# One layer's expert stage: three blocks of row gathers ranked below a product, and 112 instead of 80 of its chunks listed ahead of the gates

## The chip, the cores and the metric

The kernel runs on one core of a Trainium2 chip. The metric is the device time of one execution in microseconds (us). A core has a matrix engine (TensorE, PE in the rows; PEld is its weight load), a vector engine (VectorE, DVE), a scalar engine (ScalarE, ACT), GpSimd (POOL) and a sync engine (SyncE, SP), each working through its own list of instructions in order, and 16 DMA engines that they share.

## The reference

Two layers work on 512 latent tokens and, in the first layer only, on 256 context tokens, of 1024 features. Each layer is a mixer (attention in layer 0, two recurrences in layer 1) and then a PEER expert layer with 16384 experts, of which each token takes 16 in each of 8 heads:

```python
def block(xb):                                  # 128 tokens
    q = (xb @ w_q).reshape(T, PEER_HEADS, 2, PEER_HALF)
    s = jnp.einsum("thpd,pkd->thpk", q, sub_keys)
    sv, si = lax.top_k(s, PEER_TOPK)
    ...
    top_s, pos = lax.top_k(cand_s, PEER_TOPK)   # 16 of the 16 x 16 sums
    idx = jnp.take_along_axis(cand_i, pos, axis=-1)
    gate = jax.nn.softmax(top_s, axis=-1)
    act = jax.nn.gelu(jnp.einsum("td,thkd->thk", xb, u[idx]), approximate=False)
    return jnp.einsum("thk,thkd->td", (gate * act), v[idx])
```

The context's last state starts the recurrences of layer 1.

## The kernel before

There are six blocks of 128 tokens in layer 0: two of context, four latent. The expert layer is computed in two ways. Three latent blocks (`DENSE`) take the **dense path**: for all 16384 experts, in 128 chunks of 128 experts, `hidden` makes u.x for the 384 tokens and a GELU (24 matmuls that write `ph`; per chunk one 512 KB load `u`, its split into two parts `uh` on ScalarE, L793, and `ul` on VectorE, L794), and `peer_values` multiplies by the gates and by v into six PSUM banks `acc` (18 matmuls, a 512 KB load `v` with its split `vh`, `vl`, and the split `wl` of the gated hidden). The gates of all experts are built by `gate_grid` out of the routing: per block 32 groups of four tokens, each with comparisons `oi` on VectorE, `oj` on VectorE and ScalarE by turns (ScalarE's in L772 and L775), four matmuls `pt`, an eviction `stage`, and a 1 MB store per 16 tokens.

The two context blocks and one latent block (`REST`) take the **gather path**, `gather_run`: 128 indirect loads of u rows (512 KB each, issued by GpSimd, L722), each followed by a dot product on VectorE (L724), and then 128 loads of v rows (L731), each followed by an accumulation on VectorE into `gacc` (L736). Row buffers `grow` are five in layer 0.

In `peer_lat` the first `128 - LATE[layer]` chunks of `hidden` are listed ahead of `gate_grid`. Their result goes to memory (`Hd`, 192 KB each) and is read back by `peer_values`. The remaining `LATE[layer]` chunks are made inside `peer_values`, which takes them first. When these are done, the memory of `hidden` is given back and `ctx_states` (the context's half of layer 1: norms, gates, features, then `delta_unit` and `delta_step`) is listed with a high rank, so that it runs beside the rest of `peer_values`. It needs both context blocks finished.

The order on each engine is made at build time by a scheduler that simulates a timeline: of what is ready it takes the one with the highest rank. `high_priority(offset=-BACK)` ranks all within it far below everything else; within one rank, what was written earlier goes first.

Of the kernel before, what the change touches and what calls it, by code (L numbers as in the profile page):

```python
# [11 lines left out]
F32R = mybir.dt.float32r  # L12
BF16 = mybir.dt.bfloat16
BACK = 1 << 20
LATE = [48, 0]
GH = 2
DENSE, REST = [1, 2, 3], [0]

# [32 lines left out]
class Kern:  # L51
# [823 lines left out]
    def peer_ctx(self, R):  # L875

        layer = 0
        with R("peer_c") as keep:
            xT = keep.tile([128, KD, CTX], F32, name="xT")
            with R("peer_n") as pn:  # L880
                self.norm_mod_T(pn, self.hc, xT, *self.acol[layer][1, 1], roles=("o", "a", "a"))
            with R("peer_r") as pool:
                kT = self.peer_keys(pool, layer)
                preps = [self.gather_prep(xT, b) for b in range(NC)]
                self.gather_select(pool, self.query(pool, layer, xT), kT, preps)
                for b in range(NC):
                    with self.tc.high_priority(offset=-BACK):
                        self.gather_run(layer, preps[b], self.hc[b], 1)

    def peer_open(self):  # L890
# [25 lines left out]
    def peer_lat(self, layer, meanwhile=None):  # L916

        nc, tc = self.nc, self.tc
        nd = len(DENSE)
        n = nd * 128  # L920
        Hd = tc.dram_tile([128, 128, n], F32, name=f"Hd{layer}")
        Gd = tc.dram_tile([16, 128, n // 16, 8, 16], F32, name=f"Gd{layer}")
        with ExitStack() as er:
            es = ExitStack()
            P = lambda nm, b=1, **k: es.enter_context(tc.tile_pool(name=nm, bufs=b, reuse_waits="tile", **k))
            R = lambda nm, b=1, **k: er.enter_context(tc.tile_pool(name=nm, bufs=b, side="right", reuse_waits="tile", **k))
            pu, ph = R("dn_u", 2), R("dn_h", 2, space=PSUM)
            self.pm = Banks(P("pp", 1, space=PSUM), {"a": ("pa", 2), "t": ("pt", 2), "o": ("po", 2)})
            (xh, xl), x0 = self.xs, self.x0
            pool, pq, pg = P("peer_r"), P("peer_q"), P("gg", 2)  # L930

            def project(hp):
                ps = self.pm("a")
                w = self.rows_x(pq, self.A["peer_w_q"][layer, hp], ps[:, :n], (xh, xl), (2, 1, 1))
                for k, b in enumerate(REST):
                    self.product(ps[:, n + k * 128:n + (k + 1) * 128], w, x0[b])
                return ps

            kT = self.peer_keys(pool, layer)
            preps = [self.gather_prep(x0[b], 0) for b in REST]  # L940
            sv = [pool.tile([128, 16, 16], F32, name=f"sv{b}") for b in range(NL)]
            si = [pool.tile([128, 16, 16], U32, name=f"si{b}") for b in range(NL)]

            def route(hp):
                g, r = divmod(hp, 2 * GH)
                if r == 2 * GH - 1:
                    self.gather_route(pool, sv[nd:], si[nd:], preps, g, g * GH)

            self.peer_scores(pool, project, kT, sv, si, route)
            with tc.high_priority(offset=-(1 + layer) * BACK):  # L950
                for b, prep in zip(REST, preps):
                    self.gather_run(layer, prep, self.h[b], 0)
            pw = R("dn_w", 2)
            ahead = 128 - LATE[layer]
            with tc.high_priority(offset=-BACK):
                for i in range(ahead):
                    w = pw.tile([128, n], F32, name="hw")
                    self.hidden(layer, i, w, pu, ph, (xh, xl))
                    nc.sync.dma_start(Hd[i], w)
            for k in range(nd):  # L960
                self.gate_grid(pg, Gd, k, *self.peer_route(pool, sv[k], si[k]))
            es.close()
            def hidden(i, w):
                if i < ahead:
                    nc.sync.dma_start(w, Hd[i])
                else:
                    self.hidden(layer, i, w, pu, ph, (xh, xl))

            y = self.peer_values(layer, Gd, Hd, [self.h[b] for b in DENSE], list(range(ahead, 128)) + list(range(ahead)),
                                 hidden)  # L970
            for i in range(128 - ahead):
                next(y)
        self.px.close()
        for _ in range(ahead):
            next(y)
        if meanwhile:
            next(y)
            with tc.high_priority(offset=3000):
                meanwhile()
            next(y, None)  # L980
        else:
            with tc.tile_pool(name="fin", bufs=NL, side="right", reuse_waits="tile") as pool:
                self.done = self.final_norm(pool)
                for b in REST:
                    self.done(self.h[b], b)
                next(y)
            next(y, None)
# [713 lines left out]
```

## Time and profile before

| | us |
|---|---|
| median of 3 runs | 4478.54 (4475.19 to 4487.54) |
| the profiled execution | 4486.37 |
| its span | 4484.6 |
| TensorE busy in it | 3977.4 (89%) |
| VectorE busy | 3428.2 (76%) |
| ScalarE busy | 1786.9 (40%) |
| GpSimd busy | 1546.6 (34%) |

The profile divides the span into 40 slices and names for each engine its busy share, the clock that was granted to TensorE, and how busy the DMA engines were. Times in the rows are counted from the start of the span. The stretches used below were cut at instructions: 1274 us is the first `oi` of layer 0's gates, 1442 the end of their first third, 1650 their end, 1677 the first `vl`, 1914, 2149 and 2331 each 32 chunks of `peer_values` on, 2495 the last `vl`.

### The profile page before, as it was taken

Reading aid. Unit: us, or ns where it says so; the run is one execution under the profiler, and the core shown is the slowest. Engines: PE = TensorE matmul, PEld = TensorE weight load, DVE = VectorE, ACT = ScalarE, POOL = GpSimd, SP = SyncE. Lnnn points to the kernel's source line nnn. Section 1 sums busy time; section 2 is a strip of 40 time slices with the busy share of each in tenths; the row PEclk is TensorE's granted clock in tenths of the full one; section 3 lists DMA queues with packets and bytes.
Section 4 is the critical chain, followed back from the end, with each engine's and each line's share of the span. In section 5 each row is a group of like instructions: output and inputs, shape, how many; then the busy total and the mean of one; then the engine's idle time right before and its main releaser. Section 6 shows DMA issues by size and latency. Waiting matters only on the chain. (4 is left out here: it accounts for less than half of the span.)

```text
span 4484.6 us, 63555 instructions
## 1 busy us (share of the span) xinstructions
PE 3977.4 (89%) x22484; PEld 3491.4 (78%) x22484; DVE 3428.2 (76%) x7022; ACT 1786.9 (40%) x3481; POOL 1546.6 (34%) x1252
## 2 busy tenths in 40 slices
PE   7995488798798559999999999998998899899998
PEld 5784265698798548997788768988987899888887
DVE  2349988899989988889975566674998888677555
ACT  3311144222346643334343433334333577433333
POOL 0026766655444554445530001221233334223000
PEclk9997598799999669999999999998999999999999
DMA  8748777988789999999985211122687899999765
GB/s 309 265 159 287 272 253 254 317 316 315 277 273 325 331 337 347 329 342 345 349 295 172 76 48 34 36 71 72 201 281 256 304 334 332 358 343 329 244 223 161
DMA packets 430455, 1140.21 MB, mean 254 GB/s; under 512 B 38148, under 2 KB 200324, under 8 KB 418872
## 3 DMA queue, kind: packets, MB, share of 16 engines
q1 hardware_dynamic: 280376, 574.04, 37.1%
q0 software_dynamic: 147456, 536.94, 34.4%
q10 hardware_dynamic: 2304, 25.17, 1.5%
q8 instruction: 177, 2.90, 0.3%
q14 instruction: 142, 1.16, 0.1%
HBM read 1039.01 MB, written 96.99 MB: 253 GB/s over the span
## 5 line engine op out<-in xcount | busy, mean ns | idle before, releaser
L731 POOL DMA_INDIRECT grow<-peer_v,gidx x512 | 722.6, 1411 | 833.1 <-DVE gacc L736 676.0
L722 POOL DMA_INDIRECT grow<-peer_u,gidx x512 | 663.6, 1296 | 697.4 <-DVE hid L724 433.4
L806 PE MATMUL ph<-xh,uh 128*128 128x384 f32 x2048 | 722.1, 353 | 106.6 <-ACT uh L793 84.4
L806 PE MATMUL ph<-xl,uh 128*128 128x384 f32 x2048 | 710.9, 347 | 0.6 <-DVE xl L124 0.6
L736 DVE SCALAR_TENSOR_TENSOR gacc<-grow,gw,gacc 128x1024 f32<-128x1024 f32 x508 | 658.2, 1296 | 42.3 <-DMA grow<-peer_v,gidx 38.6
L724 DVE CUSTOM_DVE_ANT_0 grow<-grow,gx 128x1024 f32<-128x1024 f32 x512 | 619.6, 1224 | 53.6 <-DMA grow<-peer_u,gidx 53.1
L793 ACT ACTIVATE uh<-u 128x1024 fp32r<-128x1024 f32 x340 | 357.8, 1056 | 509.2 <-DMA u<-peer_uT 185.4
L794 DVE TENSOR_TENSOR ul<-u,uh 128x1024 fp32r<-128x1024 f32 x340 | 415.6, 1224 | 118.3 <-ACT uh L793 95.7
L806 PEld LDWEIGHTS ph<-xh,uh 128*128 128x128 f32 x2048 | 402.4, 197 | 132.3 <-ACT uh L793 100.3
L841 PE MATMUL acc<-vl,wh 128*128 128x512 f32 x1536 | 481.9, 394 | 3.5 <-DVE vl L794 3.4
L841 PE MATMUL acc<-vh,wl 128*128 128x512 f32 x1536 | 474.9, 392 | 0.0
L841 PE MATMUL acc<-vh,wh 128*128 128x512 f32 x1536 | 422.2, 395 | 16.5 <-ACT vh L793 11.4
L808 PE MATMUL ph<-xh,ul 128*128 128x384 f32 x2048 | 409.3, 339 | 13.9 <-DVE ul L794 13.7
L806 PEld LDWEIGHTS ph<-xl,uh 128*128 128x128 f32 x2048 | 403.1, 197 | 4.4 <-DVE xl L124 1.0
L808 PEld LDWEIGHTS ph<-xh,ul 128*128 128x128 f32 x2048 | 360.0, 189 | 20.9 <-DVE ul L794 17.5
L794 DVE TENSOR_TENSOR vl<-v,vh 128x1024 fp32r<-128x1024 f32 x256 | 312.9, 1222 | 82.4 <-ACT vh L793 81.6
L793 ACT ACTIVATE wh<-w 128x384 fp32r<-128x384 f32 x256 | 134.3, 525 | 583.2 <-PE acc L841 418.2
L841 PEld LDWEIGHTS acc<-vh,wh 128*128 128x128 f32 x1536 | 287.7, 189 | 73.7 <-ACT vh L793 13.0
L780 PE MATMUL pt<-oi,oj 128*128 128x128 f32 x1536 | 243.5, 318 | 111.6 <-DVE oj L769 69.8
L841 PEld LDWEIGHTS acc<-vl,wh 128*128 128x128 f32 x1536 | 287.9, 189 | 65.5 <-DVE vl L794 6.3
L841 PEld LDWEIGHTS acc<-vh,wl 128*128 128x128 f32 x1536 | 288.8, 189 | 60.8
L793 ACT ACTIVATE vh<-v 128x1024 fp32r<-128x1024 f32 x256 | 270.8, 1059 | 141.8 <-PE acc L841 133.8
(549 smaller groups left out, 6601.0 us busy)
## 6 DMA issues: line engine op xcount, KB each, us to landing
u<-peer_uT SPq DMA_DIRECT2D x256, 512.0 KB
v<-peer_v SPq DMA_DIRECT2D x256, 512.0 KB
w<-mod_w SPq DMA_DIRECT2D x48, 1024.0 KB
Gd<-stage SPq DMA_DIRECT2D x48, 1024.0 KB
Hd<-hw SPq DMA_DIRECT2D x208, 192.0 KB
w<-Hd SPq DMA_DIRECT2D x208, 192.0 KB
u<-rec_w SPq DMA_DIRECT2D x52, 512.0 KB
g<-Gd SPq DMA_DIRECT2D x16, 1536.0 KB
```

The costliest lines, as they stand in the source:

```text
L722: nc.gpsimd.indirect_dma_start(out=u, out_offset=None, in_=A[f"peer_u{layer}"], in_offset=bass.IndirectOffsetOnAxis(ap=row(s), axis=0))
L724: nc.vector.tensor_tensor_reduce(u, u, x, 1.0, 0.0, OP.mult, OP.add, hid[:, s:s + 1])
L731: nc.gpsimd.indirect_dma_start(out=u, out_offset=None, in_=A[f"peer_v{layer}"], in_offset=bass.IndirectOffsetOnAxis(ap=row(s), axis=0))
L736: nc.vector.scalar_tensor_tensor(acc, u, w[:, s:s + 1], acc, op0=OP.mult, op1=OP.add)
L780: nc.tensor.matmul(ps[:, t * 128:(t + 1) * 128], oj[:, t], oi[:, t], start=True, stop=True)
L793: nc.scalar.activation(hi, x, AF.Copy)
L794: nc.vector.tensor_tensor(lo, x, hi.bitcast(F32), op=OP.subtract)
L806: self.nc.tensor.matmul(ps, wh[:, kd, :], b[:, kd, :], start=kd == 0 and b is xh, stop=False)
L808: self.nc.tensor.matmul(ps, wl[:, kd, :], xh[:, kd, :], start=False, stop=kd == KD - 1)
L841: nc.tensor.matmul(acc[b][f], a[:, b * 128:(b + 1) * 128], c[:, f * 512:(f + 1) * 512], start=k + t == 0, stop=k == len(chunks) - 1 and t ...
```

## The change

`LATE[0]` goes from 48 to 16, so 112 instead of 80 chunks of layer 0's `hidden` are listed ahead of the gates and pass through `Hd`. The gathers of the two context blocks and of layer 0's latent block get the rank `-2 * BACK`, below `hidden`; before, they had the rank of `hidden` and were written ahead of it. Layer 1 had that rank already and keeps it, and its `LATE` of 0.

```diff
-LATE = [48, 0]
+LATE = [16, 0]
 ...
                 for b in range(NC):
-                    with self.tc.high_priority(offset=-BACK):
+                    with self.tc.high_priority(offset=-2 * BACK):
                         self.gather_run(layer, preps[b], self.hc[b], 1)
 ...
             self.peer_scores(pool, project, kT, sv, si, route)
-            with tc.high_priority(offset=-(1 + layer) * BACK):
+            with tc.high_priority(offset=-2 * BACK):
                 for b, prep in zip(REST, preps):
                     self.gather_run(layer, prep, self.h[b], 0)
```

Counted in VectorE's list, layer 0:

| VectorE instructions | before | after |
|---|---|---|
| splits `ul` ahead of the first `oi` (16 of them of the queries) | 70 | 78 |
| from first to last `oi`: splits `ul` | 30 | 54 |
| from first to last `oi`: dot products and accumulations of gathers | 140 | 117 |
| gathers of the two context blocks ended at the last `oi` | all | all |
| dot products and accumulations of gathers after the first `vl` | 213 | 236 |
| chunks of `peer_values` begun when the last gather is accumulated | 96 | 128 |
| chunk of `peer_values` at which `ctx_states` begins | 49 | 17 |
| instructions of `ctx_states` on VectorE after the last `vl` | 83 | 22 |

VectorE in the third block of the gates, around the 72nd `oi` of 96 (`gacc` is the gathers' accumulation, `ul` the split of a chunk). Before:

```order
L769 TENSOR_TENSOR oj_13150<-oj_13150,tt_13070 128x512
L764 TENSOR_TENSOR oi_13170<-iota_112,tt_13070 128x512
L736 SCALAR_TENSOR_TENSOR gacc_3913<-grow_4265,gw_3910,gacc_3913 128x1024
L764 TENSOR_TENSOR oj_13178<-iota_112,tt_13070 128x512
L764 TENSOR_TENSOR oi_13181<-iota_112,tt_13070 128x512
L736 SCALAR_TENSOR_TENSOR gacc_3913<-grow_4268,gw_3910,gacc_3913 128x1024
```

After:

```order
L764 TENSOR_TENSOR oj_14266<-iota_112,tt_14158 128x512
L764 TENSOR_TENSOR oi_14269<-iota_112,tt_14158 128x512
L736 SCALAR_TENSOR_TENSOR gacc_3913<-grow_4241,gw_3910,gacc_3913 128x1024
L769 TENSOR_TENSOR oj_14266<-oj_14266,tt_14158 128x512
L794 TENSOR_TENSOR ul_12783<-u_12780,uh_12782 128x1024
L736 SCALAR_TENSOR_TENSOR gacc_3913<-grow_4244,gw_3910,gacc_3913 128x1024
L794 TENSOR_TENSOR ul_12817<-u_12814,uh_12816 128x1024
```

Splits of chunks stand between the comparisons, where only gathers stood.

VectorE around the 110th chunk of `peer_values` (`vl`, `wl` its splits, `w` the product with the gates, `tu` of `ctx_states`). Before:

```order
L794 TENSOR_TENSOR vl_18458<-v_18455,vh_18457 128x1024
L854 TENSOR_TENSOR w_18579<-w_18579,g8_18550 128x384
L1157 COPY_PREDICATED tu_20034<-tri_19072,pa_20170 128x32x4
L1179 COPY tu_20022<-pa_20174 128x256
L794 TENSOR_TENSOR wl_18494<-w_18484,wh_18493 128x384
L794 TENSOR_TENSOR vl_18489<-v_18486,vh_18488 128x1024
```

After:

```order
L794 TENSOR_TENSOR wl_18559<-w_18549,wh_18558 128x384
L736 SCALAR_TENSOR_TENSOR gacc_8679<-grow_8950,gw_8676,gacc_8679 128x1024
L794 TENSOR_TENSOR vl_18554<-v_18551,vh_18553 128x1024
L1179 COPY tu_20460<-pa_20682 128x256
L1179 COPY tu_20464<-pa_20689 128x256
L736 SCALAR_TENSOR_TENSOR gacc_8679<-grow_8953,gw_8676,gacc_8679 128x1024
L854 TENSOR_TENSOR w_18611<-w_18611,g8_18396 128x384
```

The last chunks had no gathers; now one or two accumulations stand in each.

VectorE at the end of `peer_values` (L870 adds it to `h`). Before:

```order
L870 TENSOR_TENSOR h2_102<-h2_102,v_19041 128x1024
L1219 TENSOR_TENSOR wd_20385<-pa_20380,gt1_19074 128x512
L869 TENSOR_TENSOR v_19057<-acc20_13552,v_19010 128x512
L869 TENSOR_TENSOR v_19057<-acc21_13553,v_19010 128x512
L1219 TENSOR_TENSOR wd_20392<-pa_20387,gt1_19074 128x512
L870 TENSOR_TENSOR h3_103<-h3_103,v_19057 128x1024
L1140 SCALAR_TENSOR_TENSOR nbt_20401<-pa_20394,gt6_19079,dec_20399 128x128 x2
```

After:

```order
L870 TENSOR_TENSOR h2_102<-h2_102,v_19137 128x1024
L869 TENSOR_TENSOR v_19153<-acc20_14640,v_19106 128x512
L869 TENSOR_TENSOR v_19153<-acc21_14641,v_19106 128x512
L736 SCALAR_TENSOR_TENSOR gacc_8679<-grow_9055,gw_8676,gacc_8679 128x1024
L870 TENSOR_TENSOR h3_103<-h3_103,v_19153 128x1024
L736 SCALAR_TENSOR_TENSOR gacc_8679<-grow_9058,gw_8676,gacc_8679 128x1024
L736 SCALAR_TENSOR_TENSOR gacc_8679<-grow_9061,gw_8676,gacc_8679 128x1024
```

The second half of `ctx_states` (`wd`, `nbt`) stood here; it is now ahead of this place, and the last accumulations of the latent block's gather have come here.

## Rows read from the trace of the kernel before

**Rows 1.** Windows: PE, PEld, DVE, ACT, POOL busy (count); granted clock, DMA share, GB/s.

```profile
953.00:1274.00 321.00, 270.29 (x1485) 260.39 (x1483) 308.75 (x1019) 101.41 (x137) 163.65 (x116) 0.95 0.84 298
1274.00:1442.00 168.00, 152.45 (x921) 148.79 (x920) 149.25 (x177) 100.31 (x211) 72.46 (x44) 0.96 0.90 304
1442.00:1650.00 208.00, 109.45 (x518) 100.76 (x518) 196.46 (x263) 126.24 (x325) 124.16 (x97) 0.66 0.98 330
1677.00:1914.00 237.00, 237.00 (x1189) 214.36 (x1188) 193.75 (x286) 87.14 (x117) 105.26 (x83) 1.00 0.94 342
1914.00:2149.00 235.00, 226.25 (x1135) 197.85 (x1134) 204.32 (x260) 97.34 (x158) 112.98 (x88) 0.97 0.94 346
2044.00:2149.00 105.00, 96.25 (x479) 79.85 (x478) 96.71 (x148) 51.45 (x97) 49.39 (x42) 0.93 0.97 365
2149.00:2331.00 182.00, 176.42 (x921) 147.40 (x920) 162.32 (x203) 73.13 (x118) 87.96 (x62) 1.00 0.93 338
2331.00:2495.00 164.00, 162.99 (x860) 138.36 (x859) 90.14 (x154) 63.92 (x108) 3.32 (x4) 1.00 0.49 155
2503.00:2601.00 98.00, 79.70 (x487) 69.89 (x485) 61.12 (x135) 44.43 (x121) 2.64 (x14) 0.91 0.19 60
3600.00:3800.00 200.00, 189.96 (x1228) 184.39 (x1226) 172.97 (x219) 152.42 (x353) 75.94 (x56) 1.00 1.00 340
```

**Rows 2.** Windows of tile `grow` (gathers): DVE busy (count), POOL busy (count), clock, DMA.

```profile
1442.00:1650.00 208.00, 121.62 (x97) 124.16 (x97) 0.66 0.98 330
1914.00:2149.00 235.00, 99.14 (x78) 110.79 (x79) 0.97 0.94 346
2149.00:2331.00 182.00, 68.98 (x54) 84.11 (x48) 1.00 0.93 338
3600.00:3800.00 200.00, 68.95 (x55) 75.94 (x56) 1.00 1.00 340
```

**Rows 3.** Windows of tile `ul` (splits): PE, PEld, DVE busy (count), clock, DMA.

```profile
1274.00:1442.00 168.00, 43.94 (x225) 38.96 (x224) 36.66 (x30) 0.96 0.90 304
1914.00:2149.00 235.00, 31.14 (x164) 27.45 (x164) 23.19 (x19) 0.97 0.94 346
2149.00:2331.00 182.00, 13.48 (x96) 12.38 (x96) 14.68 (x12) 1.00 0.93 338
3600.00:3800.00 200.00, 51.26 (x255) 43.30 (x253) 37.84 (x31) 1.00 1.00 340
```

**Rows 4.** Window of tile `ph` (hidden): PE, PEld, ACT busy (count), clock, DMA.

```profile
1677.00:1914.00 237.00, 118.24 (x648) 113.56 (x646) 13.17 (x27) 1.00 0.94 342
```

**Rows 5.** Window of tile `acc` (values): PE, PEld, DVE busy (count), clock, DMA.

```profile
1677.00:1914.00 237.00, 129.26 (x541) 101.24 (x542) 0.00 (x0) 1.00 0.94 342
```

**Rows 6.** Windows of tile `oi` (gates): PE, PEld, DVE busy (count), clock, DMA.

```profile
1442.00:1650.00 208.00, 108.17 (x512) 99.69 (x512) 44.09 (x65) 0.66 0.98 330
3600.00:3800.00 200.00, 62.90 (x471) 59.83 (x471) 38.99 (x57) 1.00 1.00 340
```

**Rows 7.** Waits in 1442:1650: who waited for whom, us in total, times, longest.

```profile
PEld pt L780 <- ACT oj L775: 67.8, 23, 4.3
```

**Rows 8.** Groups by line, PE, in 2503:2601: busy, mean ns | idle before.

```profile
L806 PE MATMUL pa<-aTl,uh 128*128 128x512 f32 x64 | 17.0, 416 | 0.0
...
L808 PE MATMUL pa<-aTl,ul 128*128 128x512 f32 x32 | 8.5, 396 | 0.0
...
L107 PE MATMUL pa<-cm,xn 128*128 128x128 f32 x16 | 3.8, 387 | 0.0
```

**Rows 9.** Timeline of PE behind the last chunk: start us, us, instruction, idle before.

```profile
2549.50 5.03 PE L806 MATMUL pa<-aTl,uh 128*128 128x512 f32 x16
...
2601.16 6.30 PE L806 MATMUL pa<-aTl,wgh 128*16 128x512 f32 x16 [4.71 <-ACT xp L1018]
```

**Rows 10.** The page, sixth part: DMA issues, with KB each.

```profile
u<-peer_uT SPq DMA_DIRECT2D x256, 512.0 KB
...
w<-Hd SPq DMA_DIRECT2D x208, 192.0 KB
```

## The prediction

> **What bounds the kernel now.** I read the windows first, stage by stage, because the busy shares of the whole span (TensorE 89%, VectorE 76%) average over stages with different limits. Layer 0's expert stage shows three of them [rows 1]. The scores (953 to 1274) are VectorE's: 308.75 us busy of 321, 96%. The gates fall into two parts. In their first third (1274 to 1442) 30 chunks of the dense path run beside them [rows 3] and TensorE is busy for 152.45 of 168 us at a clock of 0.96. [...] Then `peer_values` (1677 to 2495, 818 us) is TensorE's: 237, 226.25, 176.42 and 162.99 us, together 802.7 or 98%, while VectorE has 193.75 + 204.32 + 162.32 + 90.14 = 650.5 us and the DMA engines run at 0.93 to 0.94 of their time until the gathers end at about 2331, and at 0.49 behind that. The change takes TensorE's work from the stage that it bounds to one where it idles. Whether that pays is decided by VectorE and DMA, which are nearly full in both.
>
> **The change part by part.** *What a chunk costs TensorE.* In 1677 to 1914 it never idles, and holds 648 matmuls of `ph` [rows 4] and 541 of `acc` [rows 5]: 27 chunks of 24. Their busy times overlap (118.24 + 129.26 = 247.5 in 237 us), so I scale them: 237 x 118.24 / 247.5 = 113.2 us, 4.2 a chunk. 32 chunks are 134 us; the ends are 4.0 (all the overlap taken off `ph`) and 4.4.
>
> *The rank.* It does less than it says. In VectorE's order both context blocks' gathers still end at the last comparison. What moves are 23 dot products and accumulations of the latent block, from the gates (140 to 117) into `peer_values` (213 to 236), where they reach to the last chunk. Ahead of the scores nothing moves at all. One costs VectorE 68.98 / 54 = 1.28 us [rows 2] and moves 512 KB (0.524 MB).
>
> *Scores, +8.5 us.* 8 more splits at 36.66 / 30 = 1.22 us [rows 3], less one gather, on a VectorE that is full [rows 1]. If its waits took them in, 0.
>
> *Gates, +17 us.* The first third keeps 30 splits and loses one gather: 168 us as before. In the rest, 24 splits (29 us) replace 22 gathers (28 us): VectorE keeps its 196 us, and if it kept its pace the stretch would keep its 208. TensorE takes 24 x 4.2 = 101 us for 98.5 idle ones; but its 512 gate matmuls cost 108.17 us there and 471 of the same kind 62.90 where the clock was 1.00 [rows 6], so at full clock it needs 68 + 101 = 169 of 208. ScalarE gets 24 evictions and splits onto 126.24 us; in the stretch of layer 1 below it carried 152.42 of 200. DMA gets 24 loads and stores of 512 + 192 KB [rows 10], 17.3 MB, for 11.5 MB of gathers: 5.8 MB, 17 us at the 330 GB/s of this stretch, which is at 0.98. The nearest row with all of it together is layer 1's 3600 to 3800: in 200 us it does 57 of the comparisons [rows 6], 31 splits [rows 3] and 55 gathers [rows 2], with VectorE at 172.97, DMA at 1.00 and the clock at 1.00. This stretch has 64, 24 and about 75: 64 / 57 x 200 = 225 us, in which 11 splits too many and 13 gathers too few nearly cancel (13.4 against 16.6 us of VectorE). I take 225, +17, between 0 (VectorE's pace kept) and +34 (if a DMA that is full there cannot hide the 17 us of additional bytes either). Each chunk also puts two transfers into SyncE's queue between the gate stores, which wait for ScalarE; the loads behind them are buffered two deep, as in the first third, where TensorE still was 91% busy.
>
> *`peer_values`, -61 us.* Three floors for the whole of it. TensorE: 802.7 - 134 + 50 (the part of `ctx_states` that comes in, below) = 719. VectorE: 650.5 - 39 + 29 + 31 (about half of its 61.12 in 2503 to 2601) = 672. DMA: 237 x 342 + 235 x 346 + 182 x 338 + 164 x 155 = 249.3 MB [rows 1], less 32 loads of `u`, more 32 reads of `Hd` and 23 gathers, 250.9 MB: 734 us at 342 GB/s. That rate is not a ceiling, since 2044 to 2149 shows 365, and so I let TensorE's 719 be the low end. [...]
> Against floors I set the stretches that already look like the new ones. Chunks 1 to 32 now hold 15 chunks of hidden, 67 gathers and the start of `ctx_states`: as 1914 to 2149 did (19 splits, 78 gathers, 235 us), less four splits' products and 11 gathers: 220. Chunks 33 to 64 hold 12 splits and 55 gathers, as 2149 to 2331 (12 and 54, 182 us): 183. The last two lots of 32 look like 2331 to 2495 (164 us, TensorE full) with 54 gathers each: VectorE 90.14 + 69 = 159 us, which is 97% of 164, and 179 at the 89% that 2149 to 2331 reached; DMA 25.4 + 28.3 = 53.7 MB, 157 us. I take 177 each. Sum 757, -61; the bounds are -99 (719 us) and -13 (235 + 190 + 190 + 190).
>
> *Behind the last chunk, -22 us.* From 2503 to 2601 TensorE is busy 79.70 us; the products of layer 1 take 17.0 + 8.5 and the norms' transposes twice about 3.8 [rows 8], so about 46, with the overlaps up to 50, are the second half of `ctx_states`, which now runs ahead. What is left is a chain: norms until the first product at 2549.5, 25.5 us of products, and then the gates' product, which came at 2601.16 behind a wait of 4.71 [rows 9]. Without the rest: 46.5 + 25.5 + 4 = 76 of 98. The bounds are 0 (the norms set it alone) and -46. The latent block's last six accumulations come here now; three dense norms go ahead of that block's, which hides them. If they were late, they would cost 6 x 1.28 = 8 us.
>
> *Layer 1* keeps its code and, but for a few neighbours changed, its order: 0, within 10 us either way.
>
> **The sum.** 8.5 + 17 - 61 - 22 = -57.5 us on the profiled execution's 4486.4: 4428.9. That execution was 7.9 us above the median of the three runs, so from the median 4478.5 it is **4421**.
>
> **The rivals.** [...]
> *B, no difference: VectorE's order takes the bound.* Gathers now stand in every chunk, and each accumulation waits in line for its row. If VectorE got no further than the 82% of 1677 to 1914, `peer_values` would take 672 / 0.82 = 820 us: 8.5 + 17 + 2 - 22 = +5, 4484. Against it: in that stretch TensorE set the pace, and the next two show 87 and 89%. 11%.
> *C, more than forecast:* TensorE's floor is reached in `peer_values` (-99), the gates keep their 208 us, and the tail gives 35: 8.5 - 99 - 35 = -125, 4353. It needs VectorE at 94% for 719 us; 1442 to 1650 shows that share, but with TensorE half idle. 7%.
> *D, the tail stays:* `ctx_states` starts at chunk 17 by the list, but needs the second context block, whose gather ends with the gates; were it late, the 22 us stay: 4443, inside the forecast's own range of 4378 to 4463.
>
> **How the numbers follow.** The forecast (with D) has 72%, A 10%, B 11%, C 7%. About 0.3% is what a measurement of this kernel can tell from no change. Faster: the forecast nearly whole and C, 78%; the same: B and the forecast's edge, 12%; slower: A, 10%. The range leaves out A, most of C and the worse half of B: 4378 to 4483.
>
> **What would show it.** Gates: `pt` and `ph` mixed to the end, the clock above 0.9, the stretch at some 225 us. `peer_values`: about 757 us, VectorE near 89%, gathers to the last chunk, DMA above 0.9 throughout. The tail: no `delta_unit` between the last `acc` and the first product of layer 1, and that product's successor `wgh` about 76 us behind. I am wrong if the gates stretch beyond 250 us, if TensorE waits for `vl` or `wl` in the last 64 chunks, or if SyncE's queue holds back `v` or `Hd`.

## The result and the profile after

The changed kernel takes **4364.22 us** (median of 4 runs, 4357.14 to 4368.47), the kernel before beside it 4483.04 (4475.19 to 4491.70): a ratio of 0.9723, 95% interval 0.9707 to 0.9740, or 118.8 us less. Predicted were 4421 with a range of 4378 to 4483. The direction was right; the gain was twice the predicted one, and the time lies below the range.

The stages, cut at the same instructions on VectorE as ahead of the prediction, in two profiled executions of each kernel:

| us | before | before, again | after | after, again | mean change | predicted |
|---|---|---|---|---|---|---|
| to the first split of the scores | 952.5 | 944.0 | 943.8 | 952.4 | 0 | 0 |
| scores, to the first `oi` | 321.8 | 319.4 | 336.3 | 343.0 | +19 | +8.5 |
| gates, to the first `vl` | 402.1 | 399.3 | 406.7 | 411.8 | +9 | +17 |
| `peer_values`, to the last `vl` | 818.5 | 820.2 | 733.0 | 736.6 | -85 | -61 |
| tail, to layer 1's first gathered row | 687.2 | 682.1 | 651.6 | 653.3 | -32 | -22 |
| the rest of layer 1, to the end | 1302.4 | 1306.1 | 1284.0 | 1287.0 | -19 | 0 |

These sum to -108; between the medians of runs on the same chip it is -119 for the first pair and -116 for the second, so about 10 us are scatter of single executions.

Windows of the kernel after: the scores, the last two thirds of the gates, and `peer_values` by 32 chunks (columns as in [rows 1]).

```profile
944.00:1280.00 336.00, 299.06 (x1689) 291.57 (x1687) 317.56 (x1027) 112.93 (x153) 147.85 (x115) 0.95 0.86 301
...
1451.00:1664.00 213.00, 176.27 (x1065) 169.36 (x1064) 197.84 (x240) 154.68 (x370) 109.58 (x74) 0.90 1.01 342
1687.00:1901.00 214.00, 197.18 (x974) 170.01 (x975) 179.69 (x306) 90.20 (x149) 86.98 (x80) 0.97 0.94 352
1901.00:2088.00 187.00, 183.10 (x968) 153.55 (x967) 162.04 (x248) 82.26 (x136) 85.34 (x70) 1.00 0.93 336
2088.00:2256.00 168.00, 166.77 (x895) 142.40 (x894) 155.01 (x225) 56.05 (x93) 77.51 (x57) 1.00 0.93 340
2256.00:2420.00 164.00, 163.62 (x871) 139.52 (x870) 151.47 (x214) 58.25 (x96) 66.78 (x56) 1.00 0.93 335
```

The last of these windows for tile `grow` (VectorE and GpSimd busy, clock, DMA):

```profile
2256.00:2420.00 164.00, 69.32 (x55) 66.38 (x54) 1.00 0.93 335
```

The reader is to see the last row of the first table and this one. The last 32 chunks took 163.5 us, as they did before [rows 1], though 55 gathers now stand beside them where none stood: VectorE went from 90 to 151 us, DMA from 0.49 to 0.93, and TensorE is as full as it was. Over all 128 chunks VectorE's work has not changed (651.0 and 648.2 us busy: gathers and `ctx_states` came, splits went), TensorE's has (803.2 and 710.6 us), and TensorE's idle time rose only from 15 to 22 us.

In the last two thirds of the gates the granted clock went from 0.66 to 0.90, and TensorE from 109.45 of 208 us [rows 1] to 176.27 of 213, so that its idle time there fell from 98.5 to 36.7 us. Windows of tile `oi`, and the waits in the same stretch:

```profile
1451.00:1664.00 213.00, 79.01 (x520) 73.65 (x520) 43.53 (x65) 0.90 1.01 342
```

```profile
PEld pt L780 <- ACT oj L775: 19.1, 11, 3.1
```

520 gate matmuls cost 79.01 us for the 108.17 of 512 before [rows 6]: they now have chunks between them, in a stretch with a granted clock of 0.90 for 0.66. The wait for `oj` fell from 67.8 us [rows 7] to 19.1.

TensorE's timeline behind the last chunk, after (start, us, instruction, idle before):

```profile
2425.60 0.61 PE L841 MATMUL acc<-vh,wl 128*128 128x512 f32 x2
2442.94 1.12 PE L107 MATMUL pa<-cm,xn 128*128 128x128 f32 x4 [16.72 <-DVE xn L99]
...
2469.59 5.92 PE L806 MATMUL pa<-aTl,uh 128*128 128x512 f32 x16 [4.06 <-ACT uh L793]
...
2493.49 3.87 PE L806 MATMUL pa<-aTl,wgh 128*16 128x512 f32 x16
```

No `delta_unit` stands between the last `acc` and the products. The first of these comes 44 us behind the last `acc` (46 before), the product with `wgh` 68 us behind (97 before [rows 9]), and it no longer waits. Its longest waits ahead of the first product are for `xn`, a result of the norms on VectorE: 16.72 us, and 5.99, 5.92 and 2.81 for the next three blocks.

Layer 1, windows of tile `ph` (PE, PEld, ACT busy, count; clock, DMA): the scores, the gates and the values. Before:

```profile
3182.00:3449.00 267.00, 191.38 (x1005) 181.84 (x1006) 20.22 (x42) 0.96 0.79 264
3449.00:3842.00 393.00, 292.26 (x1516) 266.05 (x1515) 29.77 (x62) 0.98 0.95 321
...
3878.00:4461.00 583.00, 76.12 (x360) 64.86 (x360) 7.25 (x15) 1.00 0.80 274
```

After:

```profile
3071.00:3328.00 257.00, 185.67 (x998) 176.36 (x999) 19.61 (x41) 0.97 0.81 272
3328.00:3731.00 403.00, 307.96 (x1623) 283.34 (x1622) 32.50 (x68) 0.98 0.96 327
...
3766.00:4332.00 566.00, 56.61 (x264) 47.70 (x264) 5.32 (x11) 1.00 0.80 275
```

Layer 1's code is the same, but its values are made with 264 matmuls of `ph` inside, 11 chunks, instead of 360, 15 chunks. Four chunks at 4.2 us are 17 us, and the values took 17 less. The four went into the gates, where 1623 instead of 1516 stand, and the gates took 10 more. The scores, with nearly the same matmuls of `ph`, took 10 less.

### The profile page after: what moved, and what is told of

It reads as the page before. It is cut to its first block, busy times and chain, and to the rows that moved or that the text cites. A ratio compares the mean times of both kernels' runs of the same rounds, so it can differ in the third digit from the quotient of the medians.

```text
span 4355.4 us, 63744 instructions
## 1 busy us (share of the span) xinstructions
PE 3926.1 (90%) x22484; PEld 3452.8 (79%) x22484; DVE 3415.4 (78%) x7022; ACT 1783.2 (41%) x3482; POOL 1520.6 (35%) x1252
## 4 chain that ended last, share of the span: by engine, by line
PE 61%; DVE 16%; DMA 11%; issue 6%; ACT 4%; POOL 2%; SPq 0%; DVEq 0%; ACTq 0%; POOLq 0%
PE acc L841 23%; PE ph L806 8%; PE pa L806 6%; DMA u<-peer_uT 4%; DVE grow L724 4%; PE ph L808 3%; PE pa L808 3%; DMA grow<-peer_u,gidx 3%; PE pa L288 3%; DMA grow<-peer_v,gidx 2%; DVE gacc L736 2%; PE pt L780 2%; DVE ul L794 2%; PE pa L800 2%; PE pa L162 1%
## 5 line engine op out<-in xcount | busy, mean ns | idle before, releaser
L731 POOL DMA_INDIRECT grow<-peer_v,gidx x512 | 692.8, 1353 | 878.6 <-DVE gacc L736 739.7
L806 PEld LDWEIGHTS ph<-xh,uh 128*128 128x128 f32 x2048 | 402.1, 196 | 128.1 <-ACT uh L793 93.2
L841 PE MATMUL acc<-vh,wh 128*128 128x512 f32 x1536 | 409.4, 396 | 17.4 <-ACT vh L793 9.9
L780 PE MATMUL pt<-oi,oj 128*128 128x128 f32 x1536 | 211.5, 287 | 35.9 <-DVE oj L769 14.8
```

The source lines that it names most:

```text
L731: nc.gpsimd.indirect_dma_start(out=u, out_offset=None, in_=A[f"peer_v{layer}"], in_offset=bass.IndirectOffsetOnAxis(ap=row(s), axis=0))
L780: nc.tensor.matmul(ps[:, t * 128:(t + 1) * 128], oj[:, t], oi[:, t], start=True, stop=True)
L806: self.nc.tensor.matmul(ps, wh[:, kd, :], b[:, kd, :], start=kd == 0 and b is xh, stop=False)
L841: nc.tensor.matmul(acc[b][f], a[:, b * 128:(b + 1) * 128], c[:, f * 512:(f + 1) * 512], start=k + t == 0, stop=k == len(chunks) - 1 and t ...
```

## The experiments

**Theory.** `peer_values` costs what TensorE is given in it, at 4.2 us a chunk, plus some 20 us; what VectorE and DMA do beside it is free as long as it fits. The rank's part is indirect: it alters what the scheduler lists in the scores, the gates and layer 1. **Rivals**: VectorE (or the bytes) sets the pace of the chunks that now carry gathers; the rank alone makes the gain; layer 1 is faster because of what precedes it.

*The chunks without the rank* (all three gathers ranked as before; the edits here and below are against the changed kernel):

```diff
-                    with self.tc.high_priority(offset=-2 * BACK):
+                    with self.tc.high_priority(offset=-BACK):
 ...
-            with tc.high_priority(offset=-2 * BACK):
+            with tc.high_priority(offset=-(1 + layer) * BACK):
```

> 112 chunks listed ahead of the gates, the gathers' ranks as before. VectorE's list in layer 0 is nearly that of the changed kernel (129 splits instead of 132 at the last comparison, ctx_states from chunk 17, gathers to the last chunk), layer 1's list is that of before. Theory S (the stages: 32 chunks leave a stage that TensorE bounds, ctx_states ends ahead of the last chunk, and layer 1's 18 us come from a few neighbours that changed places in its list): peer_values of layer 0 within 10 us of 733, the stretch from its last chunk to layer 1's first gather within 10 us of 652, layer 1 as before, in all 4364 + 18 = about 4382. Rival R (the gathers' rank makes the gain): 4440 or more, with peer_values of layer 0 above 790.

Measured: 4393.77 us (4382.62 to 4405.12), ratio 0.9782, 0.9750 to 0.9815. Three quarters of the gain come from the 32 chunks alone: `peer_values` 727.6 us. The whole was to be 4382. What is missing against the changed kernel lies in the gates (425.8 us instead of 406.7 and 411.8), in the tail (661.2 instead of 651.6 and 653.3) and in layer 1 (1312.5 instead of 1284 and 1287); the scores are shorter (327.3 instead of 336.3 and 343.0).

*The rank without the chunks:*

```diff
-LATE = [16, 0]
+LATE = [48, 0]
```

> The gathers' ranks lowered, 80 chunks ahead of the gates as before. VectorE's list in layer 0 is that of before but for 8 splits ahead of the gates, layer 1's list is that of the changed kernel (325 splits instead of 321 at its last comparison). Theory S: layer 0's peer_values and what is behind it stay as before (818 and 687 us), layer 1 takes the 18 us less, in all about 4483 - 18 = 4465. If layer 1's 18 us were a scatter between executions: 4483. Rival R: below 4420.

Measured: 4484.98 us (4469.48 to 4491.48), ratio 0.9996, 0.9976 to 1.0016: no change, and not the 4465 expected. Layer 1 did shrink, to 1290.0 us, and the gates by 15; the scores (335.5 us, +14), `peer_values` (826.3 us, +8) and the tail (692.2 us, +5) took it back. What a new order gains in one stage it can lose in the others.

*The kernel before, once more:*

> The kernel before once more, for a second trace of it. If the 9 us that the changed kernel had gained ahead of its scores and the 18 us in layer 1 are a scatter between executions, these stretches differ by as much between the two traces of before; theory S expects layer 1 within 3 us of the first trace, and leaves the 9 us open.

Measured: 4472.94 us. Each stage behind the first 944 us agrees within about 5 us (table above; layer 1 within 3.7, where 3 was expected); the first one, which no edit touches, differs by 8.5.

*`ctx_states` in plain order*, to get the tail's share:

```diff
-            with tc.high_priority(offset=3000):
+            with tc.high_priority(offset=0):
```

> The changed kernel with ctx_states written at its own place, without the high rank: VectorE's list has 182 instead of 227 of its instructions ahead of the last chunk, and layer 1's list of before. Theory S for the stretch behind the last chunk: it is longer again, by about half of the 33 us that it had lost, layer 1 is as before, and peer_values is shorter by at most 5 us: in all 4364 + 18 + 17 = about 4399. Rival: that stretch's gain has another cause (the clock, or the gathers' end): it stays at 652 us, in all 4382.

Measured: 4365.59 us (4360.90 to 4372.01), ratio 0.9733, 0.9704 to 0.9761: the same time as the changed kernel, lower than both expectations. `ctx_states` ended 57 us behind the last `acc` instead of 4 us ahead of it, and yet the `wgh` product came only 7 us later (74.4 us behind the last `acc`; 67.7), as did the first product of layer 1 (51.5; 43.8). `peer_values` was 710.5 us instead of 733, since fewer of its matmuls were in it (970 other than `ph` and `acc` instead of 1161). Layer 1 took 1299.9 us, with 15 chunks left in its values as in the kernel before: 16 back.

*`ctx_states` ranked in between:*

```diff
-            with tc.high_priority(offset=3000):
+            with tc.high_priority(offset=1500):
```

> The changed kernel with `ctx_states` ranked in between: high enough to begin in chunk 17 and to keep layer 1's list of the changed kernel (954 gather instructions ahead of the last comparison of its gates), low enough that 40 of its VectorE instructions wait until behind the last chunk. With `ctx_states` in plain order `peer_values` took 710 us instead of 733, the tail 5 us more, and layer 1, in the older list, 16 us more. Theory (layer 1's time goes by its list and not by what precedes it; `peer_values` goes by the work of TensorE that it must carry): values 712 to 722, layer 1 1284, the whole 4345 to 4357. Rival (layer 1 was faster because `ctx_states` had ended early): layer 1 about 1300, the whole 4362 to 4372.

Measured: 4368.41 us (4360.59 to 4371.74), ratio 0.9723, 0.9696 to 0.9749: no better than the changed kernel. `peer_values` came as expected, 714.5 us, and layer 1 had its 11 chunks and 1293.8 us, between the 1284 of the theory and the 1300 of the rival, while the whole lies in the rival's range. So this run does not decide between them; two others do. With the rank alone `ctx_states` ended 102 us behind the last `acc` and layer 1 took 1290.0 us; with `LATE` 0 (next) it ended 41 us ahead of it and layer 1 took 1307.0. So layer 1's time goes with its own list and not with the end of `ctx_states`. Here the scores took 346 and the tail 662 us, 10 more each, and ate the gain.

*All 128 chunks ahead of the gates:*

```diff
-LATE = [16, 0]
+LATE = [0, 0]
```

> The changed kernel with `LATE` 0 instead of 16 in layer 0: all 128 chunks ahead of the gates, 16 x 4.2 = 67 us less for TensorE in `peer_values`; the gathers beside it stay (from 532 to 745 instead of 762). By VectorE's list only 3 more splits stand among the comparisons and 5 more between these and the first chunk, 8 at the other end. Layer 1's list is the older one here, +16 us. Theory (TensorE bounds `peer_values`, gathers are free under it down to VectorE's and the DMA engines' own floors): values 733 - 55 = 680, gates and the step to the values +30, the whole 4364 - 55 + 30 + 16 = 4355, between 4340 and 4370. Rival (with 67 us less of TensorE the bytes bound it: 250 MB at 340 GB/s are 735 us): values 725 to 735, the whole 4400 to 4412.

Measured: 4385.73 us (4370.65 to 4392.47), ratio 0.9761, 0.9728 to 0.9794; the whole lies between the two forecasts, and so does `peer_values` with 700.2 us, of which TensorE was busy for 682.5. The 700.2 are under the rival's 725, which had 250 MB at 340 GB/s; it was 241 MB at 344, so this run alone does not show that bytes have no part (the one without v rows, below, shows it for the last 64 chunks). And they are above the 680 of the theory, whose arithmetic I had wrong: TensorE's records show that only 7.2 chunks of `ph` left `peer_values` (11.0 to 3.8), not 13 or 16. 7.2 at 4.2 us are 30, measured 33. The rest of the chunks had stood ahead of it already. The window of the step from the gates to the values in this kernel:

```profile
1674.10:1707.70 33.60, 25.86 (x142) 25.22 (x143) 23.46 (x35) 12.40 (x19) 18.50 (x12) 0.95 1.04 385
```

The gates with that step took 424.3 us, 13 to 18 more than in the changed kernel, the tail 15 more (the latent block's last accumulation ended 43 us behind the last `acc`, 12 in the changed kernel), layer 1 with the older list 20 more. What `peer_values` gained is spent, and the intervals of the two ratios barely touch: no further gain lies on this side.

*More work on VectorE beside the chunks* (one additional instruction for every eighth v row):

```diff
+                if s % 8 == 0 and not (layer or stream):
+                    nc.vector.scalar_tensor_tensor(u, u, 1.0, u, op0=OP.mult, op1=OP.max)
```

> The changed kernel with a ninth accumulation on VectorE for every eight of the latent block's v rows in layer 0 (it changes no value): 16 instructions of 1.28 us in all, about 13 of them beside the last 64 chunks, +17 us on a VectorE that is busy for 306 of 331 us there, so 323 or 98%. Theory (TensorE sets the pace, VectorE's share is only what is asked of it): the last 64 chunks stay at 331 to 335 us, the whole 4360 to 4372. Rival (the prediction's reading: VectorE cannot get past the share that a row shows, here 92%): 323 / 0.92 = 351 us, the whole 4378 to 4388.

Measured: 4384.57 us. The last 64 chunks by 32, and the two groups of VectorE in them (out<-in, count, busy, mean ns):

```profile
2107.30:2271.10 163.80, 162.59 (x868) 138.72 (x867) 155.30 (x220) 55.73 (x93) 80.78 (x54) 1.00 0.93 342
2271.10:2430.40 159.30, 159.30 (x831) 135.33 (x830) 151.60 (x208) 54.39 (x89) 72.45 (x52) 1.00 0.91 331
```

```profile
L736 DVE SCALAR_TENSOR_TENSOR gacc<-grow,gw,gacc 128x1024 f32<-128x1024 f32 x102 | 130.8, 1282 | 0.9 <-DMA grow<-peer_v,gidx 0.8
...
L738 DVE SCALAR_TENSOR_TENSOR grow<-grow 128x1024 f32<-128x1024 f32 x13 | 15.8, 1218 | 0.0
```

VectorE stood at 95% of these 323.1 us, and they did not get longer; the rival's 351 is out. The load did not reach the intended 98%: the scheduler took 13 additional instructions in and put 7 accumulations behind the last chunk for them. In all VectorE was busy for 306.9 us, for 306.5 in the changed kernel, where the stretch had 331.3: the share rose because TensorE had less to do in it. So how far VectorE can be filled was not found. The whole lies where the rival put it, but not for its reason: of the 27 us over the changed kernel's first profiled execution `peer_values` has -10, the stretch ahead of the scores, where the kernels are equal, 7, the scores 6, the gates 8, the tail with its accumulations 12, layer 1 5. The changed kernel's second profiled execution has 4385.78.

*Less work on VectorE and DMA:*

```diff
-        for s in range(128):
+        for s in range(128 if layer or stream else 1):
```

> The changed kernel without 127 of the 128 loads of v rows of the latent block in layer 0 and their accumulations (that block's result is incomplete): 105 of them stood beside the last 64 chunks, 134 us of VectorE's 306 and 55 MB. Theory (TensorE sets the pace of the last 64 chunks, the gathers there cost nothing): they stay at 325 to 331 us, the whole 4350 to 4364. Rival (VectorE or the DMA engines bound them): the last 64 chunks fall to 300 us or less, the whole below 4335.

Measured: 4359.92 us. The same two lots:

```profile
2098.60:2258.30 159.70, 159.70 (x847) 136.10 (x847) 91.23 (x155) 55.66 (x90) 2.01 (x2) 1.00 0.59 185
2258.30:2421.10 162.80, 162.80 (x860) 138.93 (x860) 91.44 (x155) 56.45 (x92) 2.62 (x10) 1.00 0.50 155
```

With 124 us of VectorE's 306 and half of the traffic gone, the 64 chunks took 322.5 us, against 331.3 with all gathers and 323.1 with more than all. They go with TensorE's own counts: 1707, 1766 and 1699 matmuls, 0.189, 0.188 and 0.190 us each. So the gathers beside them cost nothing that can be seen. The first 64 chunks were not tested in this way: there the gathers stayed, and there nearly all of TensorE's idle time lies (the rows of 214 and 187 us of the kernel after).

*Half the step:*

```diff
-LATE = [16, 0]
+LATE = [32, 0]
```

> Half the step: `LATE` 32, with the new ranks. By the lists 16 chunks fewer stand in `peer_values` than before (the change: 32 fewer), and 176 instead of the changed kernel's 227 VectorE instructions of `ctx_states`. Layer 1 has a list of the older kind (13 + 2 chunks of hidden left for its values). Theory (`peer_values` costs what TensorE is given, at 4.2 us a chunk, and its idle time stays at some 15 to 20 us whatever VectorE carries): values 818 - 67 + 35 to 50 for `ctx_states` = 786 to 801, scores +14, gates +5, tail -20, layer 1 0: 4430 to 4455 on this chip. Rival (the gain comes once gathers stand in every chunk and TensorE is never without cover; here they end at chunk 108): values 760 or less, the whole 4395 to 4415.

Measured: 4439.21 us (4425.83 to 4449.10), ratio 0.9873, 0.9837 to 0.9909: within the theory's numbers, `peer_values` 780.9 a little below them. No threshold is seen.

*The changed kernel, once more:*

> The changed kernel once more, to see how far its stages scatter between two profiled executions: 4357 to 4372; values 733 within 5 us, the tail and layer 1 within 8, the scores within 10.

Measured: 4380.12 us (4374.46 to 4385.78), above the range expected, beside 4496.12 of the kernel before on this chip; ratio 0.9745, 0.9707 to 0.9783. Stages as in the table. The scores range from 335 to 346 us in the nine profiled executions with 78 splits ahead of the gates, with a mean of 340.

Put together, `peer_values` in eight kernels (chunks of `ph` and other matmuls than `ph` and `acc` counted from TensorE's records in it, 18 per chunk of `acc` left out):

| kernel | us | TensorE busy | idle | chunks of `ph` | other matmuls | gather instructions on VectorE |
|---|---|---|---|---|---|---|
| before | 818.5 | 803.2 | 15 | 43.2 | 790 | 214 |
| rank alone | 826.3 | 803.2 | 23 | 43.2 | 754 | 216 |
| half the step | 780.9 | 756.1 | 25 | 27.2 | 934 | 215 |
| chunks alone | 727.6 | 704.4 | 23 | 10.7 | 1098 | 230 |
| after | 733.0 | 710.6 | 22 | 11.0 | 1161 | 230 |
| `ctx_states` plain | 710.5 | 690.7 | 20 | 11.2 | 970 | 224 |
| no v rows | 721.3 | 705.4 | 16 | 11.2 | 1106 | 110 |
| `LATE` 0 | 700.2 | 682.5 | 18 | 3.8 | 1162 | 212 |

TensorE's idle time is 15 to 25 us in all of them, with 230 gather instructions or 110. The runs left out here fit too: 19 and 20 us with more work on VectorE and with `ctx_states` in between, 16 and 20 in the second executions of the kernel before and after.

## Why the prediction was right in direction and wrong in size

**The step that failed** is the one for the last two lots of 32 chunks: "VectorE 90.14 + 69 = 159 us, which is 97% of 164, and 179 at the 89% that 2149 to 2331 reached [...] I take 177 each". They took 168 and 163.5. The 89% was what VectorE had been asked for while TensorE set the pace (176.42 of 182 us [rows 1]); I used it as the most that VectorE can give. With more asked it went to 92%, and to 95% with the additional instructions. The prediction used this very argument against its rival B ("in that stretch TensorE set the pace") and not against itself. The first two lots came near: 214 to 218 and 187 for the 220 and 183 forecast. The whole was -85 for -61. What the runs show in place of that step: a lot that TensorE fills stays as long as TensorE's own work, with VectorE at 92 to 95% beside it as with VectorE at 57% (the run without v rows).

The same rows had a better answer. TensorE's floor was given as 719, and its idle time in `peer_values` was 818 - 803 = 15 us; 719 + 15 = 734, measured 733.0 and 736.6. That it fits so well is in part luck: TensorE was busy for 710.6 us, 8 less than the 719, and idle for 22, 7 more than the 15. The 719 was used as a low end only, since VectorE's floor, 672, seemed to need 94% of it. VectorE was busy for 648 us. By the records only 16 more gather instructions stood in it (six of the 23 came behind the last chunk). `ctx_states` did bring its 31 us: its instructions there last 60.8 us in sum instead of 27.3. But the forecast added whole durations, and in the records VectorE's instructions overlap where one follows the other, as this accumulation of the kernel before and the split behind it do, by 0.09 us (start us, us):

```profile
1205.28 1.28 DVE L736 SCALAR_TENSOR_TENSOR gacc<-grow,gw,gacc 128x1024 f32<-128x1024 f32 x1
1206.47 1.23 DVE L794 TENSOR_TENSOR ul<-u,uh 128x1024 fp32r<-128x1024 f32 x1
```

In all of `peer_values` durations of 707.5 us made 651.0 us busy before, and 720.8 made 648.2 after.

**Layer 1, 0 forecast, -19 measured.** That it "keeps its code and, but for a few neighbours changed, its order" was wrong in the order, and the list could tell it without a run: in VectorE's list 325 instead of 321 splits stand ahead of the last comparison of its gates. Six of the twelve profiled executions left 15 chunks to its values and took 1292 to 1313 us, 1303 in the mean; six left 11 and took 1284 to 1294, 1288 in the mean: 15 us, though single executions overlap. That this is near the 17 that four chunks cost is luck. By the stages of these twelve traces the values are 18 us shorter in the mean with 11 chunks, but the gates 13 longer: TensorE was already busy for 364 of the 393 us there, so the moved chunks give back some 5 us. Most of the gain, 11 us, lies in the scores, and why these are shorter was not found. Nor was it found why the scheduler lists layer 1 in one of two ways: the rank alone brings the shorter list of the values, and with the rank `LATE` 32, `LATE` 0 or `ctx_states` in plain order undo it, `ctx_states` ranked in between does not.

**The tail, -22 forecast, -32 measured.** The mechanism was right: the `wgh` product had followed the end of `ctx_states`. The `wgh` product was forecast at 76 us behind the last chunk, for 98, and came at 68 (97 before). The end of `ctx_states` stops to matter well ahead of where it is now: ends of +95 and +102 us behind the last `acc` put `wgh` at 97 and 104, ends of +66, +57 and +47 at 75, 74 and 76, ends of +13, +9 and -4 at 68, 64 and 68. In all of these but the first two `wgh` comes 23 to 26 us behind the first product (52 and 57 there), where the prediction took 29.5. What is left of the differences lies ahead of the first product. It came at 40 us without the latent block's accumulations (no v rows), at 44 where they end at +12 (the changed kernel), at 51 to 53 where they end at +19 to +25 (`ctx_states` in between, in plain order, more work on VectorE), and at 61 where they end at +43 (`LATE` 0), which puts `wgh` at 85. That the accumulations are the cause was not tested by itself; with `LATE` 32, where they end long before, it came at 49. The prediction put their cost at 8 us "if they were late"; in the changed kernel it is at most the 3 to 4 us over the run without v rows.

**The gates, +17 forecast, +9 measured.** Chunks and comparisons mixed, and the granted clock rose from 0.66 [rows 1] to 0.90. No run shows the slower case A, which has 10% among the chances: with the gates 9 us longer the whole was 118.8 us shorter. The stretch behind the first third took 212 to 213 us for the 225 taken, near the end "VectorE's pace kept" (208), so its +17 came out as +4. The first third, forecast unchanged, took 171 and 178 us for 168 and 165, and the step to the first `vl` some 4 less; why the first third is longer was not tested. The additional bytes, priced at up to 17 us, were carried by a DMA share of 1.01 and 342 GB/s for 0.98 and 330 [rows 1].

**The scores, +8.5 forecast, +19 measured.** VectorE's work rose as forecast, by 8.8 us (308.75 to 317.56), but its idle time rose too, from 12 to 18 and 25 us, where the prediction put nothing. The wait that grew is that of the splits for ScalarE's `uh`, before and after:

```profile
DVE ul L794 <- ACT uh L793: 5.9, 4, 2.1
...
DVE ul L794 <- ACT uh L793: 17.9, 14, 4.2
```

The second executions show 4.5 and 23.2. It comes with the rank: the rank alone has 17.4, the chunks alone 7.1. Why `uh` comes later was not tested. The eight chunks of hidden that came in with the splits were already counted as chunks that leave `peer_values`, so 10 us of their gain were lost here.

**The chances.** What came is nearest to rival C (TensorE's floor in `peer_values`, gates that keep their time, a larger tail: 4353), which had 7% and was left outside the range. Its time is met in part by luck: `peer_values` stayed 14 us above C's floor, scores and gates cost 20 us more than C had, and layer 1 brought 19 us that C did not have. Its condition, VectorE at 94%, was worked out from the overestimated 672 us; 648 of 733 are 88%. B and D did not happen.

## What to carry to other kernels

A busy share seen in a stretch that another engine bounds is what was asked for, not what can be had (VectorE's 89% here became 92% when more was asked of it): add the moved work to the bound engine's floor, add the idle time that this engine showed in the same stage, and let another engine take the bound only when its own sum of work comes out larger (here VectorE went to 95% in the last 64 chunks; beyond that nothing was tried). Work moved from a stage that TensorE fills to one where it waits is paid at the price of the matmuls that really move (with `LATE` 0 7.2 chunks at 4.2 us, 30 us, for 33 measured), so count them by stage in the records and not by the constant in the code; moved to a stage that TensorE nearly fills, as in layer 1 with 364 of 393 us, it gives little back, some 5 us of 18. When a scheduler makes the order, count the moved instructions in every later stage too: here 19 of about 110 us came from a layer that the diff sets no number of.

## What the runs showed of the hardware

With more work on VectorE this engine ran at 95% of a 323.1 us stretch, beside a TensorE at 99.6% (321.89 us) and DMA engines at 0.91 to 0.93. A matmul took 0.190 us of the stretch (0.188 in the changed kernel, 0.189 without the v rows), an accumulation 1282 ns (1279 in the changed kernel), and the core moved 342 and 331 GB/s (340 and 335).

Gate matmuls cost 211 ns in a stretch at a granted clock of 0.66 (108.17 / 512) and 152 ns at 0.90 (79.01 / 520): with the chunks of another product between them the clock was higher and they were 29 us cheaper in all, which pays part of the chunks.

In the step from the gates to the values with `LATE` 0 the core moved 385 GB/s for 34 us at a DMA share of 1.04 (a share above 1 shows that the measure is rough; over 213 us of the gates the changed kernel has 1.01). The kernel before held 365 GB/s for 105 us [rows 1]. Over all of `peer_values` the changed kernel moved 341 GB/s.
